# Preparation's key rows and inverse in tiles of their own, on diagonal 32x32 blocks, half of it behind each step's outputs

## The chip, the core and the metric

The kernel runs on one core of a Trainium2 chip. The time is device microseconds of one execution, the median of several runs. Engines are named as in the profile: PE (matrix multiply; PEld is its weight load), DVE (vector), ACT (scalar), POOL (GpSimd), and SP, which in this kernel issues nearly all DMAs, one after the other in a fixed order.

## The reference, cut to what matters

One layer mixes two groups of heads. Group A is attention over cached and new keys. Group B is a recurrence (RWKV-7) in two directions over 1024 latent tokens and 256 context tokens, 16 heads of size 64:

```python
def step(S, inp):
    r_t, w_t, k_t, v_t, kk_t, b_t = inp
    sa = jnp.einsum('bhvk,bhk->bhv', S, -kk_t)
    S = S * w_t[:, :, None, :] + sa[..., None] * b_t[:, :, None, :] + v_t[..., None] * k_t[:, :, None, :]
    return S, jnp.einsum('bhvk,bhk->bhv', S, r_t)
s_final, y = lax.scan(step, s0.astype(F32), xs, reverse=reverse)
```

Both groups are gated, joined, projected by `w_out`, added to the input and normalized.

## The kernel before, in words

**First phase** (to about 1240 us in the profile): the input projection in tiles, and beside it, for each pair of heads, segment of 256 tokens and direction, the operands of the recurrence. `gram` (L445) makes one tile `km`: for each chunk of 32 tokens and each head 64 rows of 128 numbers. Its upper 32 rows per head belong to the key rows k, its lower 32 to the rows b that multiply `sa`. Two DMAs (L460) write it to the DRAM scratch `kt`; `km` has one buffer, so the next `gram` waits until both have landed. The operands r and kk go to the scratch `ra`.

**Inverses.** Within a chunk the 32 values `sa` depend on each other through a triangular 32x32 matrix. `inverse` (L722) loads these matrices for four pairs and one segment (128 of them, tile `aw`, 16 DMAs at L728), solves them in 31 double steps on POOL (L736, L738), and writes the result to DRAM, `td` (L740). There are ten. The first runs at the end of the first phase, the others inside the second, ahead of need: `fill` calls as many POOL steps as `INVA` (4 ticks) of lead ask for.

**Second phase** (`mix_phase`, to about 2305 us): the recurrence runs chunk by chunk, 80 ticks; two chunks are a part, so there are 40 parts. Four pairs run at once, as two duos w = 0, 1 of two pairs each. Per part and duo two tiles exist twice (slot j % 2): `L`, the weights, with rows 0:64 from `ra`, 64:96 the keys and 96:128 the b rows from `kt`; and `R`, with rows 0:64 the state, 64:96 the values, 96:128 the `sa` values. A tick (`step`, L897) does, in this order:

- FST, 32 small products on rows 0:96 (L911, `bank0`), which ACT copies into rows 96:128 of `R` (L918);
- UPD, 32 products on all 128 rows (L931, `bank1`), which DVE scales by the decay tile `wc` into the next state (L942);
- OUT, 32 products (L955), the outputs, copied by ACT (L960) and stored.

So that rows 96:128 need not be solved in the tick, each part is prepared beforehand: `prep` (L798) multiplies the b rows of `L` by the inverse `Tb`, 16 products per duo of a 32x32 weight block with 96 columns. All four blocks q lie in rows 96:128 and in four different column blocks (`tile_position=(96, 32 * q)`). Its result in the PSUM bank `yb` goes back into rows 96:128 of `L` by four ACT copies (L808). Both duos of part j + 1 are prepared in the second tick of part j: duo 0 after `fill(0)`, duo 1 at the tick's end. `load_part` (L768) fetches part j + 1 at the start of part j: `L` from `kt` (L774), `Tb` from `td` (L795, one buffer, `TBUF`), `R` from `vb` (L783) and `L` from `ra` (L784).

**The order.** Attention runs between these pieces: `fill` draws score products (L1077, `sc`), transposes (L1107, `pa`) and value products (L1122, `po`), projections and norms. The order in each engine's queue is made when the program is built, by a scheduler with a modelled timeline; `ahead(500)` gives FST, UPD and OUT precedence, and a list `chain` fixes the order of their products among each other. At run time each queue runs strictly in that order, and a DMA of SP that must wait for a buffer holds all DMAs behind it. The decay tile `wc` (two in all, one for each half of the heads) has two buffers (L844).

## Time and profile before

| | us |
|---|---|
| median of 3 runs | 2568.41 (2560.18 to 2575.65) |
| the profiled execution | 2572.84 |
| its span | 2570.8 |
| PE busy | 2320.6 (90%) |
| DVE, ACT, POOL busy | 1480.2, 1221.3, 1138.7 |
| DMA packets | 518009, 437.53 MB |
| mean granted clock of PE | 0.944 |

The profiled execution is the one whose rows are shown; it lies 4.4 us above the median. A row of waits has the engine and line that waited, what it waited for, the total, the number of waits and the longest one. A row of the timeline has the start, the length, the engine, line, operation and tiles, how many were merged, and in brackets the idle time before it and what ended it. Matmul counts in the trace are twice those in the code, since each product in float32 is recorded as two.

### The profile page before, as it was taken

What the parts mean: (1) busy time and instruction counts of PE and PEld (TensorE: products, weight loads), DVE (VectorE), ACT (ScalarE), POOL (GpSimd) and SP (SyncE); (2) the same over time, 40 slices, a digit from 0 to 9 for tenths busy, and PEclk for the clock granted to TensorE, in tenths of its full rate; (3) what the DMA queues carried; (4) which work ended last, traced back from release to release, by engine and by line L of the source; (5) the groups of instructions that cost most, each with busy time, mean ns of one, the idle gap of its engine ahead of it and who ended that gap; (6) DMA issues with size and microseconds to landing.
All of it is one profiled execution on the core that took longest, in us unless ns stands there. A gap on an engine that the chain in (4) does not pass through costs nothing.

```text
span 2570.8 us, 60369 instructions
## 1 busy us (share of the span) xinstructions
PE 2320.6 (90%) x23907; PEld 1891.8 (74%) x23907; DVE 1480.2 (58%) x2950; ACT 1221.3 (48%) x2528; POOL 1138.7 (44%) x1665
## 2 busy tenths in 40 slices
PE   6999999999999999999688899888998989997886
PEld 4788888888888888788466776666767767775675
DVE  5665574646455755533356676575745544565677
ACT  3333444334333433322366676576645655572353
POOL 4244344242442443448176776545665211033374
PEclk9999999999999999999789899898889999998998
DMA  7455656565645564565989796988869779777435
GB/s 243 110 150 135 188 140 174 138 164 161 163 137 156 137 177 119 153 165 152 229 186 200 159 189 130 178 172 200 172 139 244 193 182 214 182 197 241 141 120 181
DMA packets 518009, 437.53 MB, mean 170 GB/s; under 512 B 157831, under 2 KB 462131, under 8 KB 512608
## 3 DMA queue, kind: packets, MB, share of 16 engines
q1 hardware_dynamic: 515632, 427.94, 66.9%
q0 software_dynamic: 2096, 5.75, 1.2%
q8 instruction: 188, 3.08, 0.5%
q14 instruction: 93, 0.76, 0.1%
HBM read 258.69 MB, written 163.86 MB: 164 GB/s over the span
## 4 chain that ended last, share of the span: by engine, by line
PE 51%; DMA 18%; POOL 10%; DVE 7%; SPq 5%; issue 5%; ACT 4%; POOLq 0%; DVEq 0%; ACTq 0%
PE sc L1077 4%; PE po L1122 3%; DMA L<-kt 3%; PE pg L451 3%; POOL tt L738 2%; PE bank L931 2%; POOL tmp L736 2%; PE pa L1107 2%; PE yb L805 2%; DMA yn<-y 2%; PE pso L1330 2%; DMA acc<-acc 2%; PE pso L1332 2%; PE pso L1331 2%; PE ptk L455 1%
## 5 line engine op out<-in xcount | busy, mean ns | idle before, releaser
L1077 PE MATMUL sc<-ka,q 128*128 128x512 f32 (+1 forms) x832 | 294.8, 448 | 33.6 <-DVE pb L1080 26.3
L1085 ACT ACTIVATE pb<-pb,mn 128x1536 f32<-128x1536 f32 (+1 forms) x160 | 218.1, 1364 | 107.4 <-DVE pb L1080 99.8
L1080 DVE TENSOR_SCALAR_CACHE_REDUCE pb<-sc,mn 128x512 f32<-128x512 f32 x256 | 191.5, 748 | 130.8 <-PE sc L1077 113.0
L1122 PE MATMUL po<-vk,aT 128*128 128x128 f32 x1600 | 228.3, 287 | 4.5 <-ACT aT L1109 4.4
L736 POOL TENSOR_TENSOR tmp<-aw,tt 128x31 f32<-128x31 f32 (+15 forms) x310 | 166.7, 538 | 140.0 <-DMA aw<-kt 60.5
L1122 PEld LDWEIGHTS po<-vk,aT 128*128 128x128 f32 x1600 | 212.5, 200 | 20.5 <-ACT aT L1109 6.2
L481 POOL TENSOR_SCALAR ta<-ta,ka 128x256 f32<-128x256 f32 x80 | 87.7, 1097 | 293.2 <-DVE bk L479 293.1
L458 ACT COPY km<-ptk 64x256 f32<-64x256 f32 x320 | 117.4, 367 | 188.1 <-PE ptk L455 162.8
L738 POOL TENSOR_TENSOR tt<-tt,tmp 128x31 f32<-128x31 f32 (+15 forms) x310 | 183.9, 593 | 20.4
L1077 PEld LDWEIGHTS sc<-ka,q 128*128 128x128 f32 x832 | 139.2, 201 | 70.0 <-DVE pb L1080 37.8
L1099 DVE SCALAR_TENSOR_TENSOR pb<-pb,cc,pb 128x512 f32<-128x512 f32 (+1 forms) x208 | 165.0, 840 | 2.0
L808 ACT COPY L<-yb 32x384 f32<-32x384 f32 x312 | 146.4, 469 | 41.1 <-PE yb L805 36.1
L942 DVE TENSOR_TENSOR R<-bank,wc 64x256 f32<-64x256 f32 x312 | 131.1, 420 | 58.2 <-PE bank L931 49.3
L1080 DVE TENSOR_SCALAR_CACHE_REDUCE pb<-sc 128x512 f32<-128x512 f32 (+1 forms) x160 | 100.9, 634 | 102.4 <-PE sc L1077 95.4
L452 DVE TENSOR_TENSOR km<-pg,msk 128x512 f32<-128x512 f32 x80 | 55.1, 688 | 179.0 <-PE pg L451 162.7
L805 PE MATMUL yb<-L,Tb 32*32 32x96 f32 x2496 | 107.5, 263 | 53.0 <-DMA Tb<-td 26.9
L1107 PE MATMUL pa<-ident,pb 128*128 128x128 f32 x800 | 132.7, 293 | 24.4 <-DVE acc L1324 19.1
L1109 ACT COPY aT<-pa 128x512 f32<-128x512 f32 (+1 forms) x208 | 115.5, 570 | 71.1 <-PE pa L1107 69.1
L805 PEld LDWEIGHTS yb<-L,Tb 32*32 32x32 f32 x2496 | 64.7, 111 | 102.7 <-issue 59.5
L918 ACT COPY R<-bank 32x256 f32<-32x256 f32 x320 | 115.9, 362 | 47.8 <-PE bank L911 43.6
L1107 PEld LDWEIGHTS pa<-ident,pb 128*128 128x128 f32 x800 | 97.3, 149 | 49.1 <-DVE acc L1324 22.1
L1314 POOL TENSOR_TENSOR olo<-of,ohi 128x512 fp32r<-128x512 f32 x30 | 39.0, 1300 | 209.4 <-ACT ohi L1313 196.5
(354 smaller groups left out, 6431.2 us busy)
## 6 DMA issues: line engine op xcount, KB each, us to landing
kt<-km SPq DMA_DIRECT2D x160, 256.0 KB
L<-kt SPq DMA_DIRECT2D x80, 512.0 KB
acc<-acc SPq DMA_DIRECT2D x50, 512.0 KB
ra<-ra SPq DMA_DIRECT2D x160, 128.0 KB
L<-ra SPq DMA_DIRECT2D x80, 256.0 KB
R<-vb SPq DMA_DIRECT2D x160, 64.0 KB
y<-ys SPq DMA_DIRECT2D x160, 64.0 KB
yn<-y SPq DMA_DIRECT2D x40, 256.0 KB
```

Of the source, the lines that this page charges most:

```text
L458: nc.scalar.copy(km[64 * h:64 * h + 64, e:NC:2, 0:HD], pt[64 * e:64 * e + 64, :, 64 * h:64 * h + 64])
L736: e.tensor_tensor(mv, aw[:n, t, t + 1:CH].unsqueeze(2).broadcast_to([n, w, j]), tt[:n, t:t + 1, 0:j].broadcast_to([n, w, j]), op=ALU.mult)
L738: e.tensor_tensor(tt[:n, t + 1:CH, 0:j], tt[:n, t + 1:CH, 0:j], mv, op=ALU.add)
L805: nc.tensor.matmul(pp[32 * q:32 * q + 32, n:n + 96], Tb[96:128, e, HN * q + c, :], L[96:128, e, q // 2, q % 2, c, 0:96], start=True, stop= ...
L808: nc.scalar.copy(L[96:128, :, q // 2, q % 2, :, 0:96], pp[32 * q:32 * q + 32, 0:192 * HN].rearrange("p (e c y) -> p e c y", e=2, y=96))
L942: hold(nc.vector.tensor_tensor(dst[:, :, :, hv(h)], bank[1][hv(h), 256 * w:256 * w + 256].rearrange("p (d e v) -> p d e v", e=2, d=2), wcs ...
L1077: nc.tensor.matmul(sc, q[:, v, m, qc], ka[:, m, 0:kn], start=(v == 0), stop=(v == 1))
L1080: nc.vector.tensor_scalar(pm[:, c * 512:c * 512 + kn], sc, -0.125, mn[:, c - 1:c] if c else None, op0=ALU.mult, op1=ALU.min, accum_out=mn[ ...
L1085: soon.append(lambda: nc.scalar.activation(v, v, AF.Exp, bias=mn[:, c:c + 1], scale=-1.0, accum_out=B["l"][:, m, B["b"]:B["b"] + 1]))
L1099: nc.vector.scalar_tensor_tensor(a, B["p"][1][:, v], B["cc"], a, op0=ALU.mult, op1=ALU.add)
L1107: nc.tensor.transpose(pt[:, t * P:(t + 1) * P], B["p"][0][:, 512 * c + t * P:512 * c + (t + 1) * P], ident)
L1122: nc.tensor.matmul(po, B["aT"][c][:, t * P:(t + 1) * P], vk[:, t, :], start=(c == 0 and t == 0), stop=(c == last and t == nt - 1))
```

## The change

The lower 32 rows of `km` go to a scratch of their own, `bt`, and only the upper 32 to `kt`: four DMAs per `gram` where there were two, of half the size. `inverse` reads `bt` with 8 DMAs of 16 matrices in place of 16 DMAs of 8. `load_part` reads only rows 64:96 of `L` from `kt` and no inverse. A new `load_early` loads for one duo the b rows into a tile `Bt` and the inverse into a tile `Tb`, both laid out so that block q lies in rows 32q to 32q + 32; one buffer for each duo. `prep` takes both operands from there, block q in rows and columns 32q (`tile_position=(32 * q, 32 * q)`), and its ACT copies are a function `put`. In each tick k of part j, duo k of part j + 1 is prepared, chained behind OUT ahead of the copy of the outputs; then come its copies, and then `load_early(j + 2, k)`. `INVA` is 5. `wc` has one buffer, and its second load is called in the tick after which the first half of the heads is done, not two segments earlier.

```diff
-INVA = 4
+INVA = 5
...
-    scratch("kt", [H // 2, 5, NF, HD, 2, 2, 2, HN * P])
+    scratch("kt", [H // 2, 5, NF, CH, 2, 2, 2, HN * P])
+    scratch("bt", [H // 2, 5, NF, 2, 2, CH, 2, HN * P])
...
                 nc.sync.dma_start(s["kt"][p // 2, it, :, :, p % 2, h, d].rearrange("f r y -> r f y"),
-                                  km[64 * h:64 * h + 64].rearrange("r (f c) x -> r f (c x)", f=NF))
+                                  km[64 * h:64 * h + CH].rearrange("r (f c) x -> r f (c x)", f=NF))
+                nc.sync.dma_start(s["bt"][p // 2, it, :, h, d, :, p % 2].rearrange("f r y -> r f y"),
+                                  km[64 * h + CH:64 * h + 64].rearrange("r (f c) x -> r f (c x)", f=NF))
...
-        for f in range(NF):
-            kt = s["kt"][p // 2, sg + 1, f, CH:HD, p % 2].rearrange("t h d (c y) -> (h d c) t y", y=P)
-            u = 32 * g + 4 * HN * f
-            nc.sync.dma_start(aw[u:u + 4 * HN], kt[:, :, 96:128])
+        bt = s["bt"][p // 2, sg + 1, :, :, :, :, p % 2].rearrange("f h d t y -> (f h d) t y")
+        for c in range(HN):
+            nc.sync.dma_start(aw[32 * g + c:32 * g + 32:HN], bt[:, :, c * P + 96:c * P + P])
...
-            nc.sync.dma_start(L[64:128].rearrange("r e h d c y -> r (e h d c y)"),
+            nc.sync.dma_start(L[64:96].rearrange("r e h d c y -> r (e h d c y)"),
                               s["kt"][p // 2, sg + 1, f].rearrange("r e h d y -> r (e h d y)"))
-        load_inv(j)
...
-    def load_inv(j):
+    def load_early(j, w):
         m, f = j // NF, j % NF
-        Tb = cp.tile([P, NL, 4 * HN, CH], F32, tag="Tb", name=f"Tb{j}", bufs=TBUF)
...
+        Bt = cp.tile([P, 2, HN, P], F32, tag=f"Bt{w}", name=f"Bt{j}_{w}")
+        nc.sync.dma_start(Bt.rearrange("r e c y -> r (e c y)"),
+                          s["bt"][p // 2, sg + 1, f].rearrange("h d r e y -> (h d) r (e y)"))
+        Tb = cp.tile([P, 2, HN, CH], F32, tag=f"Tb{w}", name=f"Tb{j}_{w}")
+        src = tds[m].rearrange("t (x f q u) s -> f q t x (u s)", x=NL, f=NF, q=4)
+        for e in range(2):
+            nc.sync.dma_start(Tb[:, e].rearrange("t u s -> t (u s)"), src[f, :, :, 2 * w + e])
...
-                    nc.tensor.matmul(pp[32 * q:32 * q + 32, n:n + 96], Tb[96:128, e, HN * q + c, :],
-                                     L[96:128, e, q // 2, q % 2, c, 0:96], start=True, stop=True, tile_position=(96, 32 * q))
+                    g = slice(32 * q, 32 * q + 32)
+                    follow(nc.tensor.matmul(pp[g, n:n + 96], Tb[g, e, c, :], Bt[g, e, c, 0:96], start=True, stop=True,
+                                            tile_position=(32 * q, 32 * q)), chain)
...
-        w = wk.tile([P, NL, 5, 2, NC], F32, tag="wc", name=f"wc{p0}", bufs=2)
+        w = wk.tile([P, NL, 5, 2, NC], F32, tag="wc", name=f"wc{p0}")
...
-        if later_prep:
-            prep(j + 1, 0, yb)
...
+            if j + 1 < n_part:
+                prep(j + 1, k, yb, chain)
             nc.scalar.copy(ysb[m, g][:, k], bank[0][:, 256:512].rearrange("p (x v) -> p x v", x=NL))
+        if j + 1 < n_part:
+            put(j + 1, k, yb)
+        if j + 2 < n_part:
+            load_early(j + 2, k)
         fill(1)
-        if later_prep:
-            prep(j + 1, 1, yb)
...
+        if sg == 3 and m + 1 < n_item:
+            load_decays(m + 1)
```

What this does to the queues is seen at three places. `R01` is duo 0, slot 1; `sc1_7_1_1` a score product of head 1, block 7. **PE, before, around the first preparation of part 10**: OUT (L955), attention, the 16 products of duo 0 (L805) in three pieces, and the next FST (L911).

```order
L955 MATMUL bank0_12282<-R01_11574,L01_11573 32x64 x8
L955 MATMUL bank0_12282<-R11_11594,L11_11593 32x64 x8
L1122 MATMUL po1_5_15365<-vk_1_2_14090,aT1_5_2_15354 128x128 x4
L1107 MATMUL pa1_6_0_15456<-ident_78,pb0_12285 128x128 x4
L1107 MATMUL pa1_6_1_15507<-ident_78,pb0_12285 128x128 x4
L805 MATMUL yb_12284<-L00_11563,Tb10_15406 32x96 x7
L1077 MATMUL sc1_7_1_1_15463<-ka_1_1_13827,q_1_1_13833 128x512 x2
L805 MATMUL yb_12284<-L00_11563,Tb10_15406 32x96 x2
L1077 MATMUL sc1_7_1_2_15514<-ka_1_2_13830,q_1_1_13833 128x512 x2
L805 MATMUL yb_12284<-L00_11563,Tb10_15406 32x96 x7
L911 MATMUL bank0_12282<-R01_11574,L01_11573 32x64 x2
```

PE after the change, at duo 1 of the same part; UPD is L951 there, OUT L975, the preparation L812.

```order
L951 MATMUL bank1_12452<-R01_11727,L01_11726 64x64 x8
L951 MATMUL bank1_12452<-R11_11747,L11_11746 64x64 x8
L975 MATMUL bank0_12451<-R01_11727,L01_11726 32x64 x8
L975 MATMUL bank0_12451<-R11_11747,L11_11746 32x64 x8
L812 MATMUL yb_12453<-Bt10_1_15587,Tb10_1_15589 32x96 x16
L1099 MATMUL sc1_5_1_0_15334<-ka_1_0_12929,q_1_1_14051 128x512 x2
L1129 MATMUL pa1_4_0_15339<-ident_79,pb0_12454 128x128 x4
```

The 16 products stand in one piece behind OUT. So it is with 60 of the 78 preparations in `step`; the other 18 stand in 96 pieces with attention between. **SP, before, around the load of part 10** (`L00` is loaded from `kt` and `ra`).

```order
L783 DMA R00_11564<-vb_68 32x2x256
L774 DMA L00_11563<-kt_67 64x2048
L974 DMA y_75<-ys2_0_15168 32x2x256 x4
L774 DMA L10_11583<-kt_67 64x2048
L783 DMA R00_11564<-vb_68 32x2x256
L784 DMA L00_11563<-ra_66 64x16x64
L783 DMA R10_11584<-vb_68 32x2x256
L1171 DMA oT_72<-ga1_3_15103 128x512
L795 DMA Tb10_15406<-td2_12963 32x4x256
L783 DMA R10_11584<-vb_68 32x2x256
L784 DMA L10_11583<-ra_66 64x16x64
```

SP after, around the load of part 9 (slot 1).

```order
L797 DMA Bt9_0_15080<-bt_68 128x512
L802 DMA Tb9_0_15082<-td2_12992 128x1x64 x2
L784 DMA R01_11727<-vb_69 32x2x256
L776 DMA L01_11726<-kt_67 32x2048
L776 DMA L11_11746<-kt_67 32x2048
L797 DMA Bt9_1_15240<-bt_68 128x512
L802 DMA Tb9_1_15242<-td2_12992 128x1x64 x2
L996 DMA y_76<-ys1_3_15042 32x2x256 x4
L784 DMA R01_11727<-vb_69 32x2x256
L785 DMA L01_11726<-ra_66 64x16x64
```

One load of the inverse has become six DMAs. Three of them stand ahead of the part's loads of `L` and `R`, three among them, where before `Tb` stood near their end. **SP, before, at the start of the second phase**: attention's first loads end, then the sixteenth load of the second inverse's matrices (`aw1`; the other fifteen stand ahead of attention's loads), the first outputs, and part 2.

```order
L1050 DMA ka_0_3_12332<-khi_62 64x2x256
L1050 DMA ka_0_3_12332<-klo_63 64x2x256
L1059 DMA vk_0_3_12335<-va_64 128x2x128
L728 DMA aw1_12359<-kt_67 8x32x32
L974 DMA y_75<-ys0_0_12435 32x2x256 x4
L774 DMA L00_11563<-kt_67 64x2048
L774 DMA L10_11583<-kt_67 64x2048
L795 DMA Tb2_12581<-td0_77 32x4x256
```

SP after, at the same place; all eight loads of `aw1` stand ahead of attention's loads.

```order
L1072 DMA ka_0_3_12501<-klo_63 64x2x256
L1081 DMA vk_0_3_12504<-va_64 128x2x128
L797 DMA Bt2_0_12642<-bt_68 128x512
L802 DMA Tb2_0_12644<-td0_78 128x1x64 x2
L797 DMA Bt2_1_12732<-bt_68 128x512
L802 DMA Tb2_1_12734<-td0_78 128x1x64 x2
L996 DMA y_76<-ys0_0_12604 32x2x256 x4
```

The early loads of part 2 stand directly behind attention's first loads, ahead of the outputs.

More of the change, by code (lines that the diff above doesn't have):

```diff
@@ L787, in mix_phase, with prep @@
     tds = {0: td0}
-    Tbs = {}
-    def load_inv(j):
+    early = {}
+    def load_early(j, w):
         m, f = j // NF, j % NF
-        Tb = cp.tile([P, NL, 4 * HN, CH], F32, tag="Tb", name=f"Tb{j}", bufs=TBUF)
-        src = tds[m].rearrange("t (x u) s -> t x u s", x=NL)[:, :, 4 * HN * f:4 * HN * (f + 1)]
-        nc.sync.dma_start(Tb[96:128].rearrange("t x u s -> t x (u s)"), src.rearrange("t x u s -> t x (u s)"))
-        Tbs[j] = Tb
-    def prep(j, w, pp):
-        L = slots[w, j % 2][0]
-        Tb = Tbs[j][:, 2 * w:2 * w + 2]
+        p0, sg = items[m]
+        p = p0 + 2 * w
+        Bt = cp.tile([P, 2, HN, P], F32, tag=f"Bt{w}", name=f"Bt{j}_{w}")
[5 more added lines that the diff above has]
+            nc.sync.dma_start(Tb[:, e].rearrange("t u s -> t (u s)"), src[f, :, :, 2 * w + e])
+        early[j, w] = (Bt, Tb)
+    def prep(j, w, pp, chain):
+        Bt, Tb = early.pop((j, w))
         for e in range(2):
@@ L804, in prep, with put @@
                     n = 96 * (HN * e + c)
-                    nc.tensor.matmul(pp[32 * q:32 * q + 32, n:n + 96], Tb[96:128, e, HN * q + c, :],
-                                     L[96:128, e, q // 2, q % 2, c, 0:96], start=True, stop=True, tile_position=(96, 32 * q))
+                    g = slice(32 * q, 32 * q + 32)
+                    follow(nc.tensor.matmul(pp[g, n:n + 96], Tb[g, e, c, :], Bt[g, e, c, 0:96], start=True, stop=True,
+                                            tile_position=(32 * q, 32 * q)), chain)
+    def put(j, w, pp):
+        L = slots[w, j % 2][0]
         for q in range(4):
@@ L809, in prep, with follow @@
                            pp[32 * q:32 * q + 32, 0:192 * HN].rearrange("p (e c y) -> p e c y", e=2, y=96))
+    def follow(x, chain):
+        if chain:
+            tc.add_manual_dep(x.ins, chain[-1], mybir.DependencyInfo(mybir.DependencyClass.NoSync, mybir.DependencyReason.SCHED_ONLY))
+        chain.append(x.ins.name)
+    for w in duos:
+        load_early(0, w)
     for j in range(2):
@@ L815, in mix_phase @@
         yield
-        prep(0, w, psm.tile([P, 512], F32, tag="psm", name=f"pp{w}"))
+        pp = psm.tile([P, 512], F32, tag="psm", name=f"pp{w}")
+        prep(0, w, pp, [])
+        put(0, w, pp)
+    for w in duos:
+        load_early(1, w)
     yield True
@@ L840, in mix_phase, with load_decays @@
     sts, wcs = {}, {}
-    def load_pairs(m):
+    def load_decays(m):
         p0 = items[m][0]
-        w = wk.tile([P, NL, 5, 2, NC], F32, tag="wc", name=f"wc{p0}", bufs=2)
+        w = wk.tile([P, NL, 5, 2, NC], F32, tag="wc", name=f"wc{p0}")
         e = nc.sync if m else nc.gpsimd
@@ L848, in load_pairs @@
         wcs[p0] = w
+    def load_pairs(m):
+        p0 = items[m][0]
+        e = nc.sync if m else nc.gpsimd
         for x in range(NL):
@@ L892, in held @@
         whole.clear()
-        if chain:
-            tc.add_manual_dep(x.ins, chain[-1], mybir.DependencyInfo(mybir.DependencyClass.NoSync, mybir.DependencyReason.SCHED_ONLY))
-        chain.append(x.ins.name)
+        follow(x, chain)
     def step(j, k, fill):
@@ L901, in step @@
         hv = lambda h: slice(64 * h, 64 * h + 64)
-        later_prep = k == HN - 1 and j + 1 < n_part
         chain = []
@@ L956, in step @@
                                                  start=True, stop=True, tile_position=(0, q))
-                            if chain:
-                                tc.add_manual_dep(x.ins, chain[-1], mybir.DependencyInfo(mybir.DependencyClass.NoSync, mybir.DependencyReason.SCHED_ONLY))
-                            chain.append(x.ins.name)
+                            follow(x, chain)
+            if j + 1 < n_part:
+                prep(j + 1, k, yb, chain)
             nc.scalar.copy(ysb[m, g][:, k], bank[0][:, 256:512].rearrange("p (x v) -> p x v", x=NL))
+        if j + 1 < n_part:
+            put(j + 1, k, yb)
+        if j + 2 < n_part:
+            load_early(j + 2, k)
         fill(1)
-        if later_prep:
-            prep(j + 1, 1, yb)
     def store_y(m, g):
@@ L1428, in mix_phase @@
     next(att)
+    load_decays(0)
     load_pairs(0)
```

## The prediction

> **What bounds the kernel now.** First I read the busy time of each engine by phase (length, then PE, PEld, DVE, ACT, POOL busy, the granted clock, the DMA share, GB/s): the first phase, the recurrence, the tail.
>
> ```profile
> 120.00:1180.00 1060.00, 1032.86 (x8070) 874.12 (x8070) 583.03 (x892) 405.36 (x777) 421.88 (x472) 0.99 0.58 154
> 1245.00:2305.00 1060.00, 931.59 (x13394) 729.67 (x13386) 632.59 (x1524) 660.18 (x1442) 518.39 (x928) 0.91 0.84 185
> 2305.00:2571.00 266.00, 209.44 (x1167) 165.87 (x1166) 173.41 (x373) 99.85 (x212) 120.64 (x153) 0.90 0.53 172
> ```
>
> PE is the bound throughout. In the first phase it stands idle for 1060 - 1033 = 27 us, in the recurrence for 1060 - 932 = 128 us. The change acts on the recurrence, so the next view is what PE waited for there (total, times, longest).
>
> ```profile
> PE yb L805 <- DMA Tb<-td: 26.9, 8, 10.5
> PE yb L805 <- DMA L<-kt: 16.9, 5, 4.4
> PE sc L1077 <- DVE pb L1080: 14.4, 14, 3.7
> PE bank L931 <- ACT R L918: 13.3, 13, 2.0
> ...
> PE bank L911 <- ACT ys L960: 6.2, 6, 1.7
> PE yb L805 <- ACT acc L1322: 4.7, 1, 4.7
> ...
> PE yb L805 <- DMA of<-oT: 2.4, 1, 2.4
> ```
>
> The two longest rows are the preparation itself, waiting for the inverse and for the rows of `L`. With the two single waits of the same line it is 26.9 + 16.9 + 4.7 + 2.4 = 50.9 us, 2% of the span. FST (L911) never waits for a DMA: the preparation comes first and takes the wait. How such a wait arises is seen in the timeline around 1650 us.
>
> ```profile
> 1649.41 0.37 PE L805 MATMUL yb<-L,Tb 32*32 32x96 f32 x8
> ...
> 1652.39 0.58 SPq L795 DMA_DIRECT2D Tb<-td  x1
> ...
> 1657.75 0.84 PE L805 MATMUL yb<-L,Tb 32*32 32x96 f32 x26 [3.28 <-DMA Tb<-td]
> ```
>
> `Tb` has one buffer. The last preparation from it ends at 1649.8; only then can SP fetch the next one, at 1652.4; it lands 5.3 us later, and PE has stood for 3.3 us.
>
> **The change, part by part.** *The waits of the preparation.* After the change both operands of a preparation are asked for when the same duo's preparation one part earlier is over, two ticks ahead. A tick is 1060 us / 80 = 13.25 us, so the lead is 26 us against the 8.3 us from buffer to landing above. The duo's copies are a tick old when the bank `yb` is written again, so the waits behind ACT go too. Removed: 50.9 us. What is late next is looked at piece by piece.
>
> *The start.* The longest wait, 10.45 us, is that of part 2.
>
> ```profile
> 1247.49 9.13 SPq L728 DMA_DIRECT2D aw<-kt  x13
> ...
> 1279.23 0.30 SPq L728 DMA_DIRECT2D aw<-kt  x1
> ...
> 1283.45 0.60 SPq L795 DMA_DIRECT2D Tb<-td  x1
> ```
> ```profile
> 1290.64 1.50 PE L805 MATMUL yb<-L,Tb 32*32 32x96 f32 x32 [10.45 <-DMA Tb<-td]
> ```
>
> Thirteen small loads, 0.70 us each, stand ahead of attention's first loads, and `Tb` for part 2 comes behind all of them at 1283.45. After the change eight loads replace these, which saves SP about 5 us; the six early loads of part 1 take about 3 of it back; `Bt` and `Tb` of part 2 move up by four output DMAs and two of `L`, but their preparation also moves up by a tick. I let half of the wait stay: 5 us back, between 0 and 10.45. The second inverse gets its last matrices not at 1279 but with the others.
>
> ```profile
> 1335.20 1.78 POOL L740 DMA_DIRECT2D td<-tt  x1 [0.30 <-POOL tt L738]
> ...
> DMA to landing us min/median/max: 7.1/9.2/12.4
> ```
>
> It ends at 1335 now and lands some 9 us later. The first duo of part 4 wants it a tick earlier; POOL can start up to 20 us earlier. I cost that at nothing; the cover is those 20 us, and without them it costs one tick at most, 13 us.
>
> *The key rows.* `L<-kt` shrinks from 64 rows to 32 and is no longer wanted by the preparation, but by FST of its part.
>
> ```profile
> 1399.31 0.60 PE L805 MATMUL yb<-L,Tb 32*32 32x96 f32 x12 [4.39 <-DMA L<-kt]
> ...
> 1405.42 0.65 PE L911 MATMUL bank<-R,L 96*32 96x64 f32 x32
> ```
>
> Here FST ran 6.1 us after the landing, so loads may be late by as much again. PE now comes sooner by the waits that went: I give back a quarter of the 16.9 us, 4 us, between 0 and 16.9.
>
> *SP.* What its issues cost (minimum, median, maximum in ns):
>
> ```profile
> L774 SPq DMA_DIRECT2D L<-kt x80: 467/480/1292, 1202.3 to 2279.1; - x80
> L795 SPq DMA_DIRECT2D Tb<-td x40: 572/584/2159, 1220.3 to 2284.4; - x40
> L728 SPq DMA_DIRECT2D aw<-kt x160: 265/362/2359, 1131.8 to 1892.5; - x160
> L460 SPq DMA_DIRECT2D kt<-km x160: 574/581/1493, 154.7 to 1139.3; - x160
> ```
>
> Per part two `Bt` (at 0.48) and four `Tb` in place of one (at 0.584) add 2.7 us, over 38 parts 103 us; nine inverses with eight loads fewer (at 0.362) take 26 us off. SP issues for 77 us more in 1060, 7%. Beside PE's work this costs nothing unless a load is late; 5 us for that, between 0 and all 77. `Bt` also makes SP wait for a preparation; behind it queue the outputs, `L` and `R` of the part and attention's loads. The nearest row is what SP now waits for `R`'s buffer:
>
> ```profile
> SPq L783 <- PE bank L955: 47.5, 19, 8.3
> ```
>
> That is 2.5 us a time, and such waits lie inside the lead of 26 us; the slower rival below is made of them.
>
> *First phase.* 160 more DMAs of 0.58 us are 93 us of SP beside a PE that is 97% busy. `km` is released later by two issues, 1.2 us. Who waits for `km`'s stores now:
>
> ```profile
> DVE km L452: 14.3, 5
> ACT km L458: 11.3, 3
> ```
>
> Eight of 160 waits, on engines that are half idle there: 3 us, between 0 and 8 x 1.2 = 9.
>
> *Decays.* The second `wc` is asked for late, one tick ahead. The first one took 6.2 us:
>
> ```profile
> wc<-wc POOLq DMA_DIRECT2D x1, 160.0 KB, 6.2
> ```
>
> The tick hides it: 2 us, between 0 and 6.2.
>
> *The products.* The blocks lay in one row group and four column groups, and lie on the diagonal now. Rates from the timeline:
>
> ```profile
> 2223.64 0.86 PE L805 MATMUL yb<-L,Tb 32*32 32x96 f32 x32
> ```
> ```profile
> 707.14 1.15 PE L451 MATMUL pg<-ra,bk 64*64 64x64 f32 x32
> ```
> ```profile
> 2215.56 1.15 PE L931 MATMUL bank<-R,L 128*64 128x64 f32 x32
> ...
> 2216.64 0.65 PE L955 MATMUL bank<-R,L 128*32 128x64 f32 x32
> ```
>
> 32 products with 64 columns take 1.15 us in two column groups (L931) and 0.65 us in four (L955): column groups work at the same time, and the preparation already has four. `gram` (L451) works on a diagonal of two blocks in one PSUM bank and takes 1.15 us too, no longer than L931. So the diagonal changes nothing: 0 us, and the same count of products and copies. Nor does the change of shape cost much: L955 starts before the modelled end of L931. In the order, from the first to the last preparation, PE enters small shapes 313 times before and 322 times after, as FST and OUT are cut more often; chaining gains nothing there.
>
> [...]
>
> Sum: 2572.84 - 50.9 + 5 + 4 + 5 + 3 + 2 = 2541 for the profiled execution, which lies 4.4 us above its median of 2568.41. On the median: 2537 us, 1.2% faster.
>
> **The rivals.** *No change, since loads are late elsewhere.* SP and the DMA engines, with a share of 0.84 in the recurrence, are what made `Tb` late, and the change gives them more to do. If half of SP's 77 us comes back as waits of FST and of the scores for keys, the gain is 51 - 38 - 14 (the other terms but SP's) = -1: 2569. For it: FST may be free of such waits only because the preparation takes them first. Against it: most waits come from `Tb`'s single buffer, and the bytes are the same. [...]
>
> *Slower, by SP's waits for the preparation.* The place is `Bt(j + 2, k)`, behind which the loads of the next part stand. If each such wait takes 2.5 us like those for `R`, SP loses 5 us per part beyond its 2.7, and what it issues at the part's end is late. It decides once loads land over 6 us later against FST than now, the margin above. Then each of 38 part starts waits some 2.5 us: 2568 - 51 + 14 + 95 = 2626. Against it: SP's place in the order is behind the preparation's, and PE is rarely late.
>
> [...]
>
> *It doesn't do what it says*, in that 18 preparations are still cut up: that costs a change of shape each, which is priced at nothing above, so it is inside the forecast.
>
> **How the numbers follow.** A measurement of this kernel tells about 0.5%, 13 us, from no change: faster is below 2555.5, slower above 2581. The forecast, 0.62: its own range is 2513 (nothing given back and 4 us of ACT's waits gone as well) to 2553. No change, 0.20, 2557 to 2580. Slower by SP, 0.14, from 2581; by the bank, 0.04. All of the forecast is faster: 0.62, 0.20, 0.18. The range takes in the first two cases, down to 2505 for half of the 13.3 and 6.2 us that PE waits for ACT, whose copies no longer come eight in a row, and up to 2588, where the slower rival begins; about 0.18 is left out.
>
> **What would show it.** Right: no DMA among what the preparation waits for, except near the start; PE idle in the recurrence below 100 us where it was 128; 32 recorded products of a preparation in about 0.86 us; the phases around it unchanged within 5 us. Wrong: FST or scores waiting for DMAs for 30 us or more (no change); SP waiting for the preparation for over 100 us together with FST waiting for `L` (slower); preparations of 2.7 us (the bank); a wait of over 10 us for part 4's inverse near 1330 us.

## The result and the profile after

| | before | after |
|---|---|---|
| median of 4 runs, us | 2570.8 (2560.2 to 2575.7) | 2541.8 (2536.0 to 2553.0) |
| ratio, 95% interval | | 0.9898 (0.9851 to 0.9945) |
| profiled execution, span, us | 2570.8 | 2540.3 |

The kernel became 1.0% faster. In a second comparison (e10 below) the ratio was 0.9919 (0.9892 to 0.9945). The total is the one that was predicted; what it is made of is not. First the three phases, cut at the first FST and the last OUT of each kernel (length; PE, PEld, DVE, ACT and POOL busy; granted clock; DMA share; GB/s), before:

```profile
0.00:1244.10 1244.10, 1178.64 (x9315) 995.47 (x9316) 673.78 (x1053) 461.18 (x875) 498.74 (x584) 0.99 0.59 157
1244.10:2315.00 1070.90, 942.48 (x13622) 739.09 (x13622) 641.58 (x1547) 666.93 (x1457) 520.65 (x932) 0.91 0.84 185
2315.00:2570.80 255.80, 199.44 (x986) 157.25 (x974) 164.84 (x350) 93.23 (x198) 119.28 (x151) 0.89 0.52 170
```

and after:

```profile
0.00:1227.10 1227.10, 1173.44 (x9315) 990.81 (x9316) 679.87 (x1054) 463.20 (x875) 514.87 (x590) 0.99 0.61 159
1227.10:2238.10 1011.00, 879.39 (x13349) 692.94 (x13350) 610.09 (x1462) 638.38 (x1403) 489.59 (x894) 0.92 0.82 188
2238.10:2540.30 302.20, 246.79 (x1245) 196.21 (x1244) 201.86 (x436) 121.24 (x250) 144.96 (x183) 0.92 0.55 172
```

The first phase is 17 us shorter. The recurrence is 60 us shorter and the tail 46 us longer, but 273 of PE's recorded products moved from the one to the other, so the two are only compared together: 1326.7 us before, 1313.2 after, 13.5 us less. In these two PE's idle time is 128.4 + 56.4 = 184.8 us before and 131.6 + 55.4 = 187.0 after: it did not fall at all. What fell is the time in which PE is busy with the same work, 1141.9 to 1126.2 us. And that is the clock: the trace records the granted clock, and in every entry of the traces of before (76) and after (68) it is 1.0 or 0.5 of the full one. Half of the busy time under the half clock is counted as lost, an estimate: in the trace of after four score products take 2.08 us at a granted clock of 0.50 (1271.77) and 1.17 us at 1.00 (1326.68). So reckoned, PE loses 97.8 us before and 71.4 after. Without this loss its busy time did not fall but rose, from 1044.1 to 1054.8 us.

So where did the 50.9 us of waits go? The groups of the preparation, FST, UPD and the scores (busy, mean ns | idle before, and until what), before and after:

```profile
L1077 PE MATMUL sc<-ka,q 128*128 128x512 f32 (+1 forms) x832 | 294.8, 448 | 33.6 <-DVE pb L1080 26.3 <-DMA ka<-klo 6.8
L931 PE MATMUL bank<-R,L 128*64 128x64 f32 x2560 | 112.5, 237 | 14.7 <-ACT R L918 13.3 <-ACT L L808 1.0 <-issue 0.2
L805 PE MATMUL yb<-L,Tb 32*32 32x96 f32 x2496 | 107.5, 263 | 53.0 <-DMA Tb<-td 26.9 <-DMA L<-kt 16.9 <-ACT acc L1322 4.7
L911 PE MATMUL bank<-R,L 96*32 96x64 f32 x2560 | 60.3, 234 | 15.5 <-ACT ys L960 6.2 <-DVE R L942 3.6 <-issue 3.2
```

```profile
L1099 PE MATMUL sc<-ka,q 128*128 128x512 f32 (+1 forms) x832 | 296.0, 447 | 40.1 <-DVE pb L1102 34.3 <-DMA ka<-klo 4.5
L951 PE MATMUL bank<-R,L 128*64 128x64 f32 x2560 | 105.0, 239 | 29.3 <-ACT R L940 29.0
L812 PE MATMUL yb<-Bt,Tb 32*32 32x96 f32 x2496 | 94.2, 251 | 10.2 <-DMA Tb<-td 10.2
L933 PE MATMUL bank<-R,L 96*32 96x64 f32 x2560 | 72.1, 232 | 55.5 <-issue 27.3 <-DMA L<-ra 7.3 <-ACT ys L980 6.3
```

The preparation's idle time fell by 42.8 us. FST's rose by 40.0, UPD's by 14.6, the scores' by 6.5. Few of these new waits are put down to FST's own loads (`L<-ra`, 7.3 us). UPD has two long ones, 8.8 and 8.4 us; the second of these in the timeline of ACT and PE:

```profile
1300.63 0.62 ACT L1293 CAST wohi<-wst 128x512 fp32r<-128x512 f32 x1 [7.96 <-DMA wst<-w_out]
1301.27 1.91 ACT L818 COPY L<-yb 32x384 f32<-32x384 f32 x4
1303.21 0.62 ACT L1293 CAST wohi<-wst 128x512 fp32r<-128x512 f32 x1
...
1304.24 1.49 ACT L940 COPY R<-bank 32x256 f32<-32x256 f32 x4
```

```profile
1305.78 1.98 PE L951 MATMUL bank<-R,L 128*64 128x64 f32 x32 [8.41 <-ACT R L940]
```

UPD waits for ACT's copy of `R`; ACT itself stood for 8 us in front of a cast whose weights had not come, and the preparation's four copies, 1.9 us, lie ahead of the copy too. FST's longest wait has the same form, with DVE, whose queue holds the scaling into `R`:

```profile
1994.68 0.69 DVE L1023 TENSOR_TENSOR yn<-yn 128x512 f32<-128x512 f32 x1 [11.24 <-DMA yn<-y]
...
2001.25 1.72 DVE L962 TENSOR_TENSOR R<-bank,wc 64x256 f32<-64x256 f32 x4
...
2003.08 1.19 PE L933 MATMUL bank<-R,L 96*32 96x64 f32 x32 [7.89 <-issue]
```

The page calls it "issue", since it finds no releaser. The scaling, on which FST's right side depends, ends at 2002.97, 0.1 us before FST starts, behind a norm that stood for 11 us for its load. In both cases a load for another job, late, stops PE through the queue of a third engine. UPD's other long wait, at 1577 us, has the same form (ACT stood 8.3 us in front of a cast of `of`), and one of FST's, 5.6 us at 2169, nearly so (DVE stood in front of a norm, but the page names POOL for that). These four are 30.7 of the 84.8 us that FST and UPD wait after the change. In the five other waits of FST under "issue", 13.8 us, the scaling does not end last, and the profile doesn't say what did.

### The profile page after: what moved, and what is told of

It reads as the page before. It is cut to its first block, busy times and chain, and to the rows that moved or that the text cites. A ratio compares the mean times of both kernels' runs of the same rounds, so it can differ in the third digit from the quotient of the medians.

```text
span 2540.3 us, 60748 instructions
## 1 busy us (share of the span) xinstructions
PE 2299.6 (91%) x23907; PEld 1880.0 (74%) x23907; DVE 1491.8 (59%) x2950; ACT 1222.8 (48%) x2528; POOL 1149.4 (45%) x1665
## 4 chain that ended last, share of the span: by engine, by line
PE 53%; DMA 14%; POOL 9%; DVE 8%; SPq 6%; ACT 5%; issue 4%; POOLq 0%; DVEq 0%; ACTq 0%
PE sc L1099 4%; PE po L1144 4%; PE pg L452 3%; PE bank L951 3%; PE pa L1129 2%; PE yb L812 2%; DMA yn<-y 1%; PE pso L1352 1%; PE ptk L456 1%; PE bank L975 1%; PE bank L933 1%; PE psg_v L338 1%; ACT pb L1107 1%; PE psg_v L339 1%; PE psg_v L337 1%
## 5 line engine op out<-in xcount | busy, mean ns | idle before, releaser
L1107 ACT ACTIVATE pb<-pb,mn 128x1536 f32<-128x1536 f32 (+1 forms) x160 | 218.3, 1365 | 97.8 <-DVE pb L1102 94.7
L1144 PE MATMUL po<-vk,aT 128*128 128x128 f32 x1600 | 233.6, 287 | 3.7 <-ACT aT L1131 3.6
L484 POOL TENSOR_SCALAR ta<-ta,ka 128x256 f32<-128x256 f32 x80 | 93.8, 1172 | 291.3 <-DVE bk L482 287.0
L1099 PEld LDWEIGHTS sc<-ka,q 128*128 128x128 f32 x832 | 142.1, 202 | 81.7 <-DVE pb L1102 53.1
L1121 DVE SCALAR_TENSOR_TENSOR pb<-pb,cc,pb 128x512 f32<-128x512 f32 (+1 forms) x208 | 170.6, 867 | 2.0
L1131 ACT COPY aT<-pa 128x512 f32<-128x512 f32 (+1 forms) x208 | 115.1, 570 | 64.4 <-PE pa L1129 62.3
L951 PEld LDWEIGHTS bank<-R,L 128*64 128x64 f32 x2560 | 91.9, 150 | 56.4 <-ACT R L940 36.1
L951 PE MATMUL bank<-R,L 128*64 128x64 f32 x2560 | 105.0, 239 | 29.3 <-ACT R L940 29.0
```

The source lines that it names most:

```text
L951: x = nc.tensor.matmul(bank[1][hv(h), o_:o_ + 64], L[:, e, h, d, k, 0:64], R[:, k, d, e, hv(h)], start=True, stop=True, tile_position=(0, ...
L1099: nc.tensor.matmul(sc, q[:, v, m, qc], ka[:, m, 0:kn], start=(v == 0), stop=(v == 1))
L1107: soon.append(lambda: nc.scalar.activation(v, v, AF.Exp, bias=mn[:, c:c + 1], scale=-1.0, accum_out=B["l"][:, m, B["b"]:B["b"] + 1]))
L1121: nc.vector.scalar_tensor_tensor(a, B["p"][1][:, v], B["cc"], a, op0=ALU.mult, op1=ALU.add)
L1144: nc.tensor.matmul(po, B["aT"][c][:, t * P:(t + 1) * P], vk[:, t, :], start=(c == 0 and t == 0), stop=(c == last and t == nt - 1))
```

## The experiments

**Theories.** A: the prediction, the gain is the preparation's waits, removed by early loads; everything else is small. B: a good part of it comes from the first phase and has nothing to do with the preparation. C: the chain and one preparation per tick do it. D: PE's busy time depends on how often it enters a stretch of small products (FST, UPD, OUT, preparation) between the large ones, and that number is changed by anything that makes the scheduler write another order. E, a supposition that e7 and e8 test: a load whose outermost dimension is 4 is slow. All comparisons have 5 rounds, each with the kernel before on the same chip: one chip for e1 to e4, a second for e5 to e8, a third for e9 to e12. First FST, and for recurrence and tail together their length and PE's idle and busy time, are from the profiled executions. Of the busy time the last columns give the loss to the half clock, reckoned as above, and the rest, the work at full clock. Stretches are those in PE's written order from the first to the last preparation; the traces, where some products are missing, show 2 to 10 fewer.

| | median us | ratio to before, interval | first FST | recurrence + tail | idle | busy | clock loss | at full clock | stretches |
|---|---|---|---|---|---|---|---|---|---|
| before | | 1 | 1244 | 1326.7 | 184.8 | 1141.9 | 97.8 | 1044.1 | 312 |
| after | 2541.8 | 0.9898 (0.9851 to 0.9945) | 1227 | 1313.2 | 187.0 | 1126.2 | 71.4 | 1054.8 | 321 |
| e1 split stores | 2555.3 | 0.9953 (0.9926 to 0.9980) | 1226 | 1321.4 | 191.3 | 1130.1 | 87.6 | 1042.5 | 318 |
| e2 early Tb | 2590.6 | 1.0089 (1.0061 to 1.0117) | 1247 | 1330.9 | 184.1 | 1146.8 | 88.4 | 1058.5 | 354 |
| e3 old stores | 2722.5 | 1.0604 (1.0580 to 1.0627) | 1257 | 1467.3 | 278.4 | 1188.9 | 127.6 | 1061.4 | 351 |
| e4 two at once | 2526.3 | 0.9847 (0.9823 to 0.9871) | 1234 | 1287.4 | 172.2 | 1115.2 | 77.2 | 1038.0 | 301 |
| e5 no chain | 2565.3 | 0.9967 (0.9942 to 0.9993) | 1234 | 1342.3 | 157.4 | 1184.9 | 81.3 | 1103.7 | 454 |
| e6 dummy DMAs | 2604.3 | 1.0111 (1.0070 to 1.0153) | 1284 | 1323.3 | 190.8 | 1132.5 | 85.6 | 1046.9 | 312 |
| e7 four-row loads | 2605.8 | 1.0124 (1.0082 to 1.0166) | 1246 | 1355.9 | 254.5 | 1101.4 | 87.5 | 1013.9 | 210 |
| e8 Tb by blocks | 2539.6 | 0.9862 (0.9823 to 0.9901) | 1231 | 1305.4 | 174.6 | 1130.8 | 79.3 | 1051.5 | 327 |
| e9 two chained | 2516.2 | 0.9786 (0.9762 to 0.9810) | 1232 | 1282.9 | 183.7 | 1099.2 | 62.5 | 1036.7 | 276 |
| e10 after again | 2552.0 | 0.9919 (0.9892 to 0.9945) | 1232 | 1309.4 | 187.3 | 1122.1 | 66.1 | 1056.0 | 321 |
| e11 inverse later | 2556.1 | 0.9952 (0.9931 to 0.9973) | 1231 | 1317.1 | 168.0 | 1149.1 | 69.4 | 1079.7 | 382 |
| e12 two tiny DMAs | 2576.0 | 1.0002 (0.9982 to 1.0021) | 1239 | 1327.6 | 192.4 | 1135.1 | 92.6 | 1042.6 | 308 |

Two things are seen in the table as a whole. The work at full clock goes with the stretches: a straight line through the fourteen kernels rises by 0.38 us per stretch and misses them by 4 us (root mean square), where a line through the busy time itself misses by 14. And the clock's loss is 62 to 81 us in the seven kernels that load `Bt` and `Tb` early from the new scratch (after, e4, e5, e8 to e11), 86 to 98 in the five whose preparation reads `L` (before, e1, e2, e6, e12). That is not the chance of single profiles: averaged over all executions of a kernel the granted clock is 0.952 to 0.957 in the first group, 0.942 to 0.948 in the second. Beside each other on one chip it is 0.9466 for before and 0.9522 for after (e10); of 2570 us that is some 14 us, an estimate, where the medians differ by 22. Why PE is under the half clock for less time (in recurrence and tail 32 periods with 255 us before, 30 with 214 after) is not shown.

**e1: before, with the stores split.**

```diff
             for h in range(2):
-                nc.sync.dma_start(s["kt"][..., :, p % 2, h, d]..., km[64 * h:64 * h + 64]...)
+                for u in (0, CH):
+                    nc.sync.dma_start(s["kt"][..., u:u + CH, p % 2, h, d]..., km[64 * h + u:64 * h + u + CH]...)
```

> The kernel before, with one edit: each store of km is issued as two DMAs of 32 rows, into the same place, so that the first phase issues four DMAs per gram as in the kernel after; the recurrence is that of before. As a side effect the order that the scheduler writes for the first phase becomes that of the kernel after (2 of PE's 5279 rows differ from it, 2011 from before). Theory A (as predicted: the gain is the preparation's waits, the first phase gives 3 us back): 2574 us, between 0 and 9 slower than before. Theory B (17 of the 29 us that the change gained come from the first phase, whose end moved from 1244 to 1227 us, and have nothing to do with the preparation): 2554 us, first FST near 1227 us.

Measured 0.9953: 13 us less than the 2568.2 of before on that chip. Theory B; A's small loss falls. With nothing done to the preparation, some half of the change's gain is there, and the first FST runs at 1226.

**e2: before, with the inverse loaded early.**

```diff
...
-        Tb = cp.tile([P, NL, 4 * HN, CH], F32, tag="Tb", name=f"Tb{j}", bufs=TBUF)
...
+        Tb = cp.tile([P, 2, 4 * HN, CH], F32, tag=f"Tb{w}", name=f"Tb{j}_{w}")
...
             prep(j + 1, w, yb)
+            if j + 2 < n_part:
+                load_inv(j + 2, w)
```

> The kernel before, with one edit: the inverse is loaded per duo, into two tiles of half the size, as soon as the same duo's preparation of the part before is over; the rows of L, their place and the preparation's place stay. First phase in the order of before. Theory A (the waits for the inverse are time lost, and go): of 26.9 us the start's 10.45 stays in part, 20 us gained, 2551 us. Rival, that PE would have had to wait anyway (in the change 51 us of waits went and PE's idle time fell by 10): a fifth of it, 5 us gained, 2566 us.

Slower by 22 us; both theories miss, A by 40. PE's waits now:

```profile
PE sc L1084 <- DVE pb L1087: 38.5, 20, 12.4
PE yb L804 <- DMA L<-kt: 29.0, 8, 7.0
...
PE yb L804 <- DMA Tb<-td: 5.8, 1, 5.8
```

The wait for `Tb` went from 26.9 to 5.8 us as wanted, that for `L` rose from 16.9 to 29.0, that of the scores from 26.3 to 38.5. A preparation needs both operands, so bringing one early mostly hands the wait to the other. Idle time in recurrence and tail stayed (184.8, 184.1), and busy time rose by 5 us: 14 us more work at full clock, with 42 stretches more, and 9 us less of the clock's loss. The profiled execution spans 2577.6 us, 7 more than that of before, and is the fastest of e2's six. On average these six have a granted clock of 0.942, where before has 0.948 on the same chip; that is some 15 us of 2590, which can be the rest of the 22.

**e3: after, with the old stores; e7: the same, with `Bt` in four loads.**

```diff
...
-                          s["bt"][p // 2, sg + 1, f].rearrange("h d r e y -> (h d) r (e y)"))
+                          s["kt"][p // 2, sg + 1, f, CH:HD].rearrange("r e h d y -> (h d) r e y"))
```
```diff
-        nc.sync.dma_start(Bt..., s["kt"][p // 2, sg + 1, f, CH:HD].rearrange("r e h d y -> (h d) r e y"))
+        for q in range(4):
+            nc.sync.dma_start(Bt[32 * q:32 * q + 32]..., s["kt"][p // 2, sg + 1, f, CH:HD, :, q // 2, q % 2])
```

> The kernel after, with the key rows stored as before (one scratch of 64 rows, two DMAs per gram, and the inverse's matrices in 20 loads); Bt and L's 32 rows are read from it. The first phase has before's order again (2 of PE's 5279 rows differ). Theory A: 2539 us, 3 less than after. Theory B (the first phase's 17 us go back): 2558 us, first FST near 1244 us.

> The kernel with the old stores (2722 us), with one edit: Bt, which it reads from kt by one DMA whose outermost dimension is 4 (the head and direction), is read by four DMAs of 32 rows each; same bytes, same pieces of 1 KB, three more issues for SP per load, 240 in all. [...] Rival (pieces of 1 KB in place of 2 KB, or the old order of the first phase, are the cause): 2722 us or more, since nothing of that changes and SP has 240 issues more.

e3 took 2722 us, far from A and B: it tests something else. The recurrence in e3 and in e7:

```profile
1256.90:2418.80 1161.90, 939.65 (x13349) 727.70 (x13350) 604.42 (x1462) 638.37 (x1403) 484.51 (x888) 0.86 0.72 163
```

```profile
1246.40:2310.10 1063.70, 860.27 (x13372) 696.54 (x13376) 604.52 (x1466) 639.07 (x1404) 488.18 (x888) 0.90 0.82 179
```

Split into four, the same bytes in the same pieces cost 117 us less (2606; the two ran on different chips, and by the ratios it is 4.5%). That is the way theory E points; by what mechanism such a load would be slow is not shown. But E's estimate for e7 was 2560 us, and the order changed along with the edit (351 stretches, then 210). Of the recurrence's 98 us, 44 are work at full clock, which goes with the stretches, 35 the clock's loss and 19 idle time. So how much of the 117 us is the load's own was not shown. In the profiles e7 is still 62 us longer than after: 19 us in the first phase, 68 of PE's idle time behind it, less 25 of busy time. Its FST waits for `L<-ra` for 64.4 us where that of after waits for 7.3. The layout of the scratch is thus no detail: in both runs with the old one (which also has the old first phase) the early loads are a loss.

**e4: after, with two preparations in the second tick, not chained.**

```diff
+        later_prep = k == HN - 1 and j + 1 < n_part
+
+        def both(w):
+            prep(j + 1, w, yb, [])
+            put(j + 1, w, yb)
+            if j + 2 < n_part:
+                load_early(j + 2, w)
...
         fill(0)
+        if later_prep:
+            both(0)
...
-            if j + 1 < n_part:
-                prep(j + 1, k, yb, chain)
...
         fill(1)
+        if later_prep:
+            both(1)
```

> The kernel after, with both preparations of a part in its second tick at the places of before (one ahead of UPD, one at the end) and not chained; early loads and own tiles stay, first phase in the order of after. Theory A (the early loads carry the gain, the chain nothing): ACT's waits of about 5 us come back, 2546 us. Rival C (one preparation per tick, chained behind OUT, is what takes PE's waits away): the 13 us that the recurrence and the tail gained are lost, 2555 us.

Faster than after, beyond either theory: its interval ends at 0.9871, that of after in e10 begins at 0.9892. The second half of the change, one chained preparation per tick, is a loss against two at the old places. The waits of the preparation and of UPD here:

```profile
PE yb L812 <- DMA Tb<-td: 21.0, 7, 5.6
...
PE yb L812 <- DMA Bt<-bt: 12.9, 3, 6.1
...
PE bank L961 <- ACT R L948: 9.4, 8, 2.9
```

The preparation waits longer than in after, and UPD much less: in every second tick the first preparation lies between FST and UPD, in the time of ACT's copy, which would explain it. Of the 39 us by which recurrence and tail are shorter than before, 13 are idle time, 21 the clock's loss and 6 work at full clock.

**e5: after, without the chain behind OUT.**

```diff
-                prep(j + 1, k, yb, chain)
+                prep(j + 1, k, yb, [])
```

> The kernel after, with one edit: the products of the preparation hang on one another, but no longer on OUT ahead of them, so the scheduler may put other work between. In its order the preparation lies in 258 pieces where after has 156, and PE enters stretches of FST, UPD, OUT and preparation 454 times (after 321, the kernel with two preparations in the second tick 301, before 312). The early loads stay. Theory A (a change of shape costs nothing, and early loads carry the gain): 2541 us as after. Rival D (each further stretch costs PE some 0.5 to 1 us, which the kernel before with early inverse alone suggests: 42 stretches more, and 22 us slower though its waits for the inverse went): 133 stretches more than after, 67 to 133 us, 2608 to 2675 us.

The recurrence and the preparation's group:

```profile
1233.70:2269.80 1036.10, 937.85 (x13349) 704.48 (x13350) 607.61 (x1462) 640.54 (x1403) 483.79 (x890) 0.92 0.80 183
```

```profile
L812 PE MATMUL yb<-Bt,Tb 32*32 32x96 f32 x2496 | 132.5, 264 | 42.6 <-DMA Bt<-bt 22.3 <-DMA Tb<-td 17.8 <-ACT L L818 1.6
```

The same 13349 products keep PE busy for 937.9 us instead of 879.4: 58.5 us for 133 more stretches, 0.44 us each. The clock's loss is 10 of them, so the work at full clock is 48 us, 0.36 each. 38 of the 58.5 us are in the preparation itself (132.5 against 94.2). Part of that price is seen in after's timeline, where one preparation is cut in two:

```profile
1406.25 0.53 PE L812 MATMUL yb<-Bt,Tb 32*32 32x96 f32 x16
1408.10 0.53 PE L812 MATMUL yb<-Bt,Tb 32*32 32x96 f32 x16 [1.32 <-DMA Tb<-td]
```

Two halves take 1.06 us where a whole one takes 0.86. D's price is a little lower than it said (0.5 to 1 us), and its total far off: 2565 us, since PE's idle time in the recurrence fell from 131.6 to 98.3 us. Cut pieces fill waits, and give back more than half of what they cost.

**e6 and e12: is it the order of the first phase, or the stores?** In the first phase some 2010 of the 5279 rows of PE's order differ between before and after (the counts stand in the expectation of e1), though no line there was edited but the stores: the scheduler's model saw four DMAs per gram and wrote another order. e6 adds two DMAs from a constant and keeps before's order, e12 two tiny ones from `km`, with an order near that of after.

```diff
...
+            for h in range(2):
+                nc.sync.dma_start(s["dm"][h], msk[0:CH, 0, 0:HD])
```
```diff
...
+            for h in range(2):
+                nc.sync.dma_start(s["dm"][p, it, d, h], km[64 * h:64 * h + 1, 0, 0:HD])
```

> The kernel before, with two small DMAs added behind each gram's stores (32 rows of 256 bytes from a constant into a scratch that nothing reads): SP issues four DMAs per gram as with split stores, but km is stored in two pieces, and the scheduler keeps before's order in the first phase (4 of PE's 5279 rows differ). If the order that the scheduler wrote is what gained 17 us in the first phase (theory B1): 2568 to 2573 us, first FST near 1244 us or up to 4 later. If it is the count of DMAs in itself (B2): 2555 us, first FST near 1227 us.

> The kernel before, with two tiny DMAs (256 bytes from km into a place of their own that nothing reads) behind each gram's two stores; km is stored in two pieces, and is released two issues later. The scheduler writes a third order for the first phase, near that of after (340 of 5279 rows differ) and far from before's (1829). Theory B1 (the order is what gained 17 us): first FST between 1225 and 1235 us, 2555 us. Theory B2 (it is the splitting of km's stores in itself): first FST at 1244 us or later, 2570 us.

e6 was badly made: all its DMAs write one place, each waits for the one before (SP waited 69.6 us for that), and the first phase grew by 40 us. It shows how much that phase hangs on SP, and decides nothing. In e12 the first FST ran at 1239, between the two theories, and the time is that of before. The waits of DVE and ACT for `km`'s stores in e1 and in e12:

```profile
ACT km L458 <- DMA kt<-km: 8.2, 1, 8.2
DVE km L452 <- DMA kt<-km: 7.8, 1, 7.8
```

```profile
DVE km L453 <- DMA kt<-km: 21.4, 6, 7.2
...
ACT km L459 <- DMA kt<-km: 13.0, 4, 6.1
```

16 us in e1, 34 in e12, 26 before, none after. The order alone doesn't bring the gain, since e12 has nearly the same one; splitting alone was not had, since the kernels with split stores, after and e1 among them, have the other order too. That the split stores and the order that comes with them gain half a per cent is shown (e1); which of the two does it is not.

**e8: e4, with `Tb` in four loads.**

```diff
-        for e in range(2):
-            nc.sync.dma_start(Tb[:, e]..., src[f, :, :, 2 * w + e])
+        for q in range(4):
+            nc.sync.dma_start(Tb[32 * q:32 * q + 32]..., src[f, q, :, 2 * w:2 * w + 2])
```

> The kernel with two preparations in the second tick (2526 us), with one edit: Tb is loaded by four DMAs of 32 rows (one per block) in place of two whose outermost dimension is 4; 160 issues more on SP, 327 stretches in place of 301. [...] Rival (Tb is small, 32 KB a load, and latency sets it): 2526 to 2540 us.

0.9862 against 0.9847, 2539.6 us where E's estimate was 2510: no gain, as the rival said. Two rows fit latency as what sets such a load: in the trace of after the 32 KB issued at 1402.46 end PE's wait at 1408.10, 5.6 us later, and in that of before 128 KB took 5.4 us (1652.39 to 1657.75). The waits for `Tb` fell from 21.0 to 13.3 us; but PE's work at full clock rose by 13.5 us with 26 more stretches, 0.5 us each, and FST's idle time from 26.1 to 41.1 us.

**e9: e4, with the first of the two preparations chained to FST; e10: after, beside it.**

```diff
+            if later_prep:
+                prep(j + 1, 0, yb, chain)
+        if later_prep:
+            put(j + 1, 0, yb)
+            if j + 2 < n_part:
+                load_early(j + 2, 0)
         fill(0)
-        if later_prep:
-            both(0)
```

> The kernel with two preparations in the second tick (2526 us), with one edit: the first of the two hangs on the products of FST ahead of it, so that nothing is put between; UPD follows. Its order has 276 stretches of small shapes where that kernel has 301 and after 321. Theory D (a further stretch costs 0.45 us, as 133 more cost 58 us of PE's busy time without the chain): 11 us less than with two at once, 2515 us, or 0.979 of before. Rival (stretches are free, and the order alone is chance): 2526 us, 0.985 of before.

> The kernel after, unchanged, beside the others on the same chip: 0.990 of before, and slower than two chained preparations by 1% if theory D holds.

2516 us, 0.9786: the fastest of all, 1.4% under after on the same chip (2516.2 / 2552.0 = 0.986, the intervals against before far apart). Its recurrence and tail:

```profile
1232.30:2263.80 1031.50, 903.90 (x13622) 720.24 (x13622) 644.35 (x1547) 663.19 (x1457) 516.03 (x926) 0.93 0.84 193
2263.80:2515.20 251.40, 195.27 (x983) 153.77 (x972) 164.06 (x350) 92.61 (x196) 119.14 (x150) 0.91 0.53 172
```

The number is what theory D expected, the way to it is not. Against e4, in recurrence and tail, 25 stretches less go with only 1.3 us less work at full clock; the clock's loss is 15 us less and idle time 11.5 more. Against after it holds better: with 45 stretches less the work is 18 us less (0.40 each), the clock's loss 9 less and idle time 3 less.

**e11: after, with the inverses later.**

```diff
-INVA = 5
+INVA = 4
```

> The kernel after, with the inverses half a part later again, as in the kernel before (INVA 4). Its order has 382 stretches where after has 321. Theory A (as predicted: the earlier inverse costs nothing, and without it Tb comes late for the first part of an item, nine times at most 6 us): 2542 to 2570 us, the loss in the waits for Tb. Theory D: 61 stretches of 0.45 us, 27 us, 2569 us, the loss in PE's busy time at the same waits.

0.9952 against 0.9919 for after beside it: 8 us by the ratios, 4 by the medians, 7 in the two profiles, but the intervals overlap from 0.9931 to 0.9945. D's busy time came (876.7 to 900.7 us in the recurrence, 24 us for 61 stretches, 0.39 each, nearly all of it at full clock), and again idle time gave some back, 16 us. The preparation's waits for `Tb` were 13.2 us, where they were 10.2 and 4.6 in the two profiles of after.

## Why the prediction was right, and where it was wrong

**The total**, 2537 us, came out (2541.8, and in the second comparison 0.9919 of before), but by luck: the sum's large terms were wrong and nearly cancel. In the profiled executions, -30.5 us: the first phase -17.0 where +3 stood, recurrence and tail -13.5 where -50.9 + 5 + 4 + 5 + 2 = -35 stood. And the -13.5 us are not waits: idle time rose by 2.2 us, work at full clock by 10.7, and the clock's loss fell by 26.4.

**The waits of the preparation** went as said: 53.0 to 10.2 us of idle time, and of the rest 6.0 us lies near the start:

```profile
1268.70 1.50 PE L812 MATMUL yb<-Bt,Tb 32*32 32x96 f32 x32 [6.01 <-DMA Tb<-td]
...
1274.77 0.86 PE L812 MATMUL yb<-Bt,Tb 32*32 32x96 f32 x32
```

**What is late next** is the step that failed. "I give back a quarter of the 16.9 us, 4 us" was for FST's own rows. FST gave back 40 us and UPD 15. The prediction looked for a late load at the instruction that reads it; in the four long waits that were followed, 30.7 us, FST and UPD stand behind a cast or a norm in the queue of ACT or DVE, and in at least three of them that one waits for a late load. The cause of the remaining waits stays open in part. Its own sign, PE idle below 100 us in the recurrence, did not come: 131.6. By that sign the mechanism as written is wrong. The rival "loads are late elsewhere" was nearer to it, but named FST's and the scores' own loads, whose waits stayed small (7.3 us and 4.5 us, and at most 13.8 more if FST's waits without a known releaser are of that kind), and SP's extra issues as the cause.

**Products on the diagonal**, 0 us: right. The row of 1274.77 above has 32 recorded products, of four blocks of 32 in one bank, in 0.86 us, as before. The rival by the bank (0.04) stood on a preparation of 2.7 us, a term that no run shows: in the trace of after those in one piece take 0.86 us at the full clock and up to 1.50 where the granted clock is lower, and that rival falls.

**Changes of shape at nothing, "chaining gains nothing there"**: wrong. A stretch costs some 0.38 us of PE's work at full clock (the line through all kernels; 0.36 in e5, whose edit is the chain alone). It hardly showed in the total because after has only nine stretches more than before, some 3 of the 10.7 us by which that work rose; what the other 7 are stays open. One preparation per tick without the chain would have had 454 stretches, 0.5% slower than after (e5 against e10), so the chain is needed by that placement; two per part at the old places need it less and are faster (e4, e9). The placement, with the chain as it stands, costs the change 0.5 to 1.3% against e4 and e9.

**SP, 5 us**, and the slower rival: the new wait is small, and the old one shrank:

```profile
SPq L797 <- PE yb L812: 31.6, 13, 6.0
...
SPq L784 <- PE bank L975: 28.1, 12, 9.5
```

31.6 us is far below the 100 that the rival needed, and FST waited 7.3 us for `L<-ra`. The start and part 4's inverse: no wait over 6.0 us, and none near 1330 (a preparation at 1329.45 does not wait); but the earlier inverse, costed at nothing, is worth some 4 to 8 us (e11), if anything, and not through the wait that was named. The decays, 2 us: no wait for `wc` is left, before had one of 5.6 us.

**First phase, +3**: wrong in sign. Its waits for `km`'s stores went to none, where longer ones were priced; and the order there was taken as unchanged, since its code was. e1 shows the gain, 13 us. The sign "the phases around it unchanged within 5 us" did not come either.

**The clock** was in no term. The waits of PE and the granted clock around that first wait, after:

```profile
1262.00:1268.70 6.70, 0.70 (x24) 0.58 (x21) 3.83 (x5) 1.42 (x2) 6.07 (x9) 0.63 0.99 225
1268.70:1272.00 3.30, 3.30 (x73) 2.74 (x74) 1.03 (x3) 1.71 (x4) 2.99 (x5) 0.50 0.40 92
1274.00:1277.00 3.00, 1.63 (x40) 1.25 (x38) 0.64 (x2) 2.35 (x5) 2.61 (x6) 1.00 1.16 168
```

Within this wait of 6 us the granted clock goes to 0.50, at 1263.7, and it stays there until 1274.0, 5 us after PE goes on: the preparation takes 1.50 instead of 0.86 us. Over the whole execution the mean clock is 0.944 before and 0.954 after. In PE's busy time the loss fell from 111.9 to 81.7 us: 30.2 us, as much as the whole gain of the profiled pair. This pair shows it too large, since its execution of before has one of the lower clocks; by the averages of e10's comparison it is an estimated 14 of 22 us. So some half of the gain or more is time at the half clock, for which the prediction has no term. That it comes with the early loads from the new scratch is seen in seven kernels; by what route is not shown.

**Small slips** that bear on nothing: by the rows shown it is 8.0 us from the buffer to the landing of `Tb` (1649.78 to 1657.75), not 8.3; and the low end, with half of ACT's waits gone, works out to 2508 (2568.4 - 50.9 - 9.75), not 2505.

## What to carry to other kernels

When a wait is removed, look for the next late load in every in-order queue that feeds the critical engine, not only at the instruction whose operand came late; a wait of both of two operands goes only when both come early. Where a scheduler writes the order, any edit, a split DMA even, rewrites phases that it does not touch: compare the order and the number of stretches of small products before pricing the edit, and price a stretch. Before explaining a change of PE's busy time, take out what the half clock costs: here the busy time fell while the work in it rose. A change of several parts is worth taking apart even when it succeeds: here the placement gave back a third or more of what the rest gained (0.9898 against 0.9847 and 0.9786).

## What the runs showed of the hardware that was not expected

- Entering a stretch of small products on parts of the array between large ones costs PE some 0.38 us of busy time at full clock (slope over fourteen kernels with 210 to 454 stretches; 48 us for 133 in e5). A single pair of kernels can miss it: 25 stretches less in e9 than in e4 made only 1.3 us. Cutting one preparation of 32 recorded products in two costs 0.20 us.
- The half clock is a large and movable part of PE's busy time: 97.8 us of the 1141.9 in recurrence and tail before, 71.4 of 1126.2 after, though PE's idle time is the same (184.8 and 187.0). Nor is it chance of one execution: the mean granted clock is 0.947 over 28 executions of before and 0.952 over 11 of after.
- Four 32x32 blocks on the diagonal, all into one PSUM bank, take 0.86 us for 32 products in the trace of after (1274.77), as four blocks in one row group do in that of before (2223.64).
- A load of 256 KB with an outermost dimension of 4, replaced by four with 32, made the kernel 117 us faster (2722 to 2606, on two chips), but with 141 stretches less, so that the load's own share is not known; for loads of 32 KB the same gained nothing (e8).
